# Scores of multi-head latent attention in two full passes and shared 32-row passes

## The chip, the cores and the metric

The kernel runs on one core of one Trainium2 chip. A core has TensorE (PE, the matrix unit, with a separate row PEld for loading its stationary operand), VectorE (DVE), ScalarE (ACT), GpSimd (POOL) and SyncE (SP, whose queue issues most DMAs here). The engines run side by side and wait for each other by semaphores; each works through its own instructions in order. Matmuls write to PSUM, which has eight banks of 128 partitions x 512 float32 values; everything else lies in SBUF, 128 partitions wide. The metric is the time of the whole kernel on the device in microseconds, the median of several runs.

## The reference: what is computed

Two transformer layers over 512 tokens of width 1024, each followed by a squared-ReLU MLP, and a final norm. The first layer has two attentions side by side, A (grouped-query) and B (multi-head latent). The change is in B. Its queries and keys are 96 wide: 64 without positions, and 32 with rotary positions, where the key's 32 are the same for all 8 heads.

```python
qb = (rmsnorm(cq, b_q_norm) @ b_w_uq).reshape(b, s, B_HEADS, B_NOPE + B_ROPE)      # 64 + 32
q_nope, q_rope = jnp.split(qb, (B_NOPE,), axis=-1)
q_rope = axial_rope(q_rope, row, col)
kvb = (rmsnorm(ckv, b_kv_norm) @ b_w_ukv).reshape(b, s, B_HEADS, B_NOPE + B_V)
k_nope, vb = jnp.split(kvb, (B_NOPE,), axis=-1)
k_rope = axial_rope(kr[:, :, None, :], row, col)
q_full = jnp.concatenate([q_nope, q_rope], axis=-1)
k_full = jnp.concatenate([k_nope, jnp.broadcast_to(k_rope, (b, s, B_HEADS, B_ROPE))], axis=-1)
ob = block_attention(q_full, k_full, vb, (B_NOPE + B_ROPE) ** -0.5)
```

`block_attention` is a softmax over all 512 keys. All is float32.

## The kernel before

Activations lie transposed, features on partitions and the 512 tokens along the free axis. TensorE multiplies in a rounded format, so the kernel splits each operand into a high part (rounded, by ScalarE) and a low part (the rest, by VectorE) and adds three products: high by high, high by low, low by high. `mm3` (lines 607 to 609) is these three matmuls for a projection.

PSUM is divided by tags: three banks `mm` for projections, two banks `s` for scores, two `t` for transposes, one `o` for attention outputs. A new tile of a tag takes a bank of that tag that is free.

`attend` (line 1095) goes through the heads, 8 of A and then 8 of B, with four query tiles of 128 for each. For a tile, `scores` (line 1127) multiplies queries by keys in a bank `s` (line 1131), VectorE takes the scaled row minimum and copies (line 1135), ScalarE takes the exponential (line 1137), VectorE the reciprocal of the sum (line 1138), and GpSimd scales (line 1139). Three tiles later `transpose` turns the four 128x128 blocks of the tile in a bank `t` (line 1106); ScalarE copies out the high part (line 1108) and VectorE the low part (line 1109), which empties the bank. When two tiles are turned, `values` multiplies them by the values in bank `o` (line 1119). After a head, `fold` adds the two halves of the output and splits pairs of heads.

Between tiles, `step` runs some microseconds of fill: a queue of projections, written as generators. During A it holds the rest of the input projection and then `projB(0)`, which makes q, k and v for the first four heads of B (parts `q0`, `k0`, `v0`). At tile 35 it receives the first output projection (three column blocks out of A's outputs), `projB(1)`, and the other output projections (3 and 2 column blocks). An output projection multiplies k = 0, 1 for all its columns and then k = 2, 3 column by column, and adds each column to the residual on VectorE (line 1065).

In `projB` a head pair's projection comes out with one head on partitions 0 to 63 and the other on 64 to 127. DMAs on SP's queue move them: the second head down to its own tile (lines 997 and 1019), and the rotary 32 rows below each head's 64 (lines 1000 and 1021). So a head's queries and keys take 96 partitions, high and low part side by side, and `passes` of `heads_B` (line 1184) gives the three products of 96 rows.

The order of instructions is written out by hand only in the opening and in the second layer's attention C. In `attend`, in the output projection and in the MLPs a planner orders each engine's instructions before the run: by program order as the priority, by an instruction's readiness in its own reckoning, with tiles given out as banks come free. So instructions of a later tile or of the fill may stand ahead of earlier ones. On the chip the order is fixed.

Of the kernel before, what the change touches and what calls it, by code (L numbers as in the profile page):

```python
# [35 lines left out]
def encoder_kernel(ctx: ExitStack, tc: tile.TileContext, ins, out, dbg=None):  # L36
# [36 lines left out]
        def free(self):  # L73
            give(self.i)

    def bank(tag, bufs):
        return ps.tile([P, 512], F32, tag=tag, bufs=bufs, name=nm(tag))

    def mmb():
        return bank("mm", 3)  # L80

    def sbk():
        return bank("s", 2)

    def stb():
        return bank("t", 2)

    def ob():
        return bank("o", 1)

    def scratch(dt=F32):
        return scp.tile([P, 512], dt, tag="sc", name=nm("sc"))
# [822 lines left out]
    def rotary_load():  # L915
        raw = hold["rawr"] = Slot(F32)
# [55 lines left out]
    def projB(g, last):  # L972
# [4 lines left out]

        def q_part():
            CQ = [s_.pair() for s_ in cqS]
            banks = three(3)  # L980
            for m in (2, 0, 1):
                for k in range(3):
                    hi, lo = (z[:, k % 2, m * P : (m + 1) * P] for z in weights(iq[k // 2]))
                    mm3(banks[m], hi, lo, CQ[k][:, 0, :], CQ[k][:, 1, :], k == 0, k == 2)
                    yield MM3
                if m == 2:
                    qc = scratch()
                    ACT.activation(qc, banks[2], AF.Copy)
# [12 lines left out]
            stg.free()  # L1001
            if last:
                for s_ in cqS:
                    s_.free()

        def k_part():
            CK = [s_.pair() for s_ in ckS]
            banks = three(2)
            for m in range(2):
                for k in range(2):  # L1010
                    hi, lo = (z[:, k, m * P : (m + 1) * P] for z in weights(iv))
                    mm3(banks[m], hi, lo, CK[k][:, 0, :], CK[k][:, 1, :], k == 0, k == 1)
                    yield MM3
                kn = scratch()
                DVE.tensor_tensor(kn, banks[m], hold["skvb"].t[:, 0:512], op=ALU.mult)
                K.extend(Slot() for _ in range(2))
                ka, kb = K[2 * m].pair(), K[2 * m + 1].pair()
                split(kn, ka)
                SP.dma_start(f32(kb[0:64, :, :]), f32(ka[64:128, :, :]))
                for k_ in (ka, kb):  # L1020
                    SP.dma_start(f32(k_[64:96, :, :]), f32(kst.pair()[0:32, :, :]))
            if last:
                kst.free()
                hold["skvb"].free()
                rpB.free()

# [68 lines left out]
    def attend(heads, step):  # L1095
# [29 lines left out]
                h["after"]()  # L1125

        def scores(h, i):
            s = sbk()
            pl = h["passes"](i)
            for n, (lh, rh) in enumerate(pl):  # L1130
                PE.matmul(s, lh, rh, start=n == 0, stop=n == len(pl) - 1)  # L1131
            h["done"](i)
            t = tiny(4)
            p = pp.tile([P, 512], F32, tag="p", name=nm("p"))
            DVE.tensor_tensor_reduce(p, s, zeros.to_broadcast([P, S]), op0=ALU.add, op1=ALU.min, scale=h["scale"](i),
                                     scalar=3e38, accum_out=t[:, 1:2])
            ACT.activation(p, p, AF.Exp, bias=t[:, 1:2], scale=-1.0, accum_out=t[:, 2:3])
            DVE.reciprocal(t[:, 3:4], t[:, 2:3])  # L1138
            POOL.tensor_scalar(p, p, t[:, 3:4], 1.0, op0=ALU.mult, op1=ALU.mult)  # L1139
            return p  # L1140

        for h in heads:
            for i in range(4):
                ripe = list(late_v)
                p = scores(h, i)
                if len(late_t) == 3:
                    transpose(*late_t.pop(0))
                late_t.append((h, i, p))
                if ripe:
                    values(*late_v.pop(0))  # L1150
                step(h, i)
        for x in late_t:
            transpose(*x)
            while late_v:
                values(*late_v.pop(0))
            fill.run(1.5)
# [20 lines left out]
    def heads_B(g):  # L1177
# [3 lines left out]
        for j in range(4):  # L1181
            q, k = Q[j].pair(), K[j].pair()

            def passes(i, q=q, k=k):
                ts = slice(i * P, (i + 1) * P)
                return [(q[0:96, 0, ts], k[0:96, 0, :]), (q[0:96, 1, ts], k[0:96, 0, :]),
                        (q[0:96, 0, ts], k[0:96, 1, :])]

            def done(i, j=j):
                if i == 3:  # L1190
                    Q[j].free()
                    K[j].free()
# [6 lines left out]
            yield dict(e=j % 2, done=done, after=after, scale=lambda i: hold["scB"][:, i : i + 1], passes=passes,  # L1199
                       vlhs=lambda kt, j=j: vv[kt // 2][:, kt % 2, j, :])  # L1200
# [10 lines left out]
    def step(h, i):  # L1211
# [869 lines left out]
```

## Time and profile before

| what | value |
|---|---|
| median of 3 runs | 1157.25 us (1157.03 to 1159.0) |
| the profiled execution's own time | 1158.44 us |
| its span | 1156.7 us |
| granted TensorE clock, mean | 0.998 |
| busy: PE / DVE / ACT / POOL | 1144.4 / 905.6 / 668.7 / 579.5 us |
| attention B in the span | scores from 144 to 228 us |

In the views that follow, a row of a timeline has the start, the duration, the engine, the line of the kernel, the instruction, what it writes `<-` what it reads (`s`, `t`, `o`, `mm` are PSUM tiles, `a` a slot of SBUF, `p` the softmax's tile, `whi`/`wlo` split weights), the shapes, and a count; in square brackets stands the idle time before it and what ended it. A row of groups has the count, then the busy time, the mean of one in ns, and the idle time before. `96*128 96x512` is a matmul with 96 rows of contraction and 512 columns. Matmuls overlap, so their durations are longer than their distance.

### The profile page before, as it was taken

The page shows a single profiled execution, that of the slowest core. Times are in us where ns is not written, and L with a number is a line of the kernel's source. Part 1 is how long each engine was busy: PE and PEld are TensorE (multiplying, and loading weights), DVE is VectorE, ACT ScalarE, POOL GpSimd, SP SyncE. Part 2 cuts the span into 40 slices and gives each one's busy share as a digit, 9 for nine tenths or more (in the row PEclk, how much of TensorE's full clock was granted, in tenths as well). Part 3 has the DMA queues.
Part 4 walks back from the last instruction along what each step waited for, and adds up shares of the span by engine and source line. Part 5 has one row for each costly group of instructions (what it writes and reads, how often), then busy time and mean ns, then how long its engine had stood idle before and what let it go on. Part 6 is the DMA issues. An engine that isn't in the chain of part 4 may idle for free.

```text
span 1156.7 us, 20518 instructions
## 1 busy us (share of the span) xinstructions
PE 1144.4 (99%) x7348; PEld 1022.1 (88%) x7348; DVE 905.6 (78%) x1576; ACT 668.7 (58%) x1135; POOL 579.5 (50%) x711
## 2 busy tenths in 40 slices
PE   9999999999999999999999999999999999999997
PEld 7787788888899999899988998988889999989996
DVE  6887988888877787978784666667996788698875
ACT  6677777755346668534453555555552666773445
POOL 4366252226688892378402232231388789535730
PEclk9999999999999999999999999999999999999999
DMA  7322415222523335933536574433344233372332
GB/s 234 95 79 71 106 51 142 65 64 80 169 92 96 88 99 140 270 105 101 155 92 164 143 182 127 119 108 119 101 155 128 74 90 94 74 192 70 121 121 73
DMA packets 115349, 134.36 MB, mean 116 GB/s; under 512 B 9795, under 2 KB 96752, under 8 KB 115248
## 3 DMA queue, kind: packets, MB, share of 16 engines
q1 hardware_dynamic: 110896, 120.09, 35.2%
q0 software_dynamic: 4032, 12.60, 5.4%
q8 instruction: 58, 0.95, 0.3%
q14 instruction: 43, 0.35, 0.1%
q10 hardware_dynamic: 320, 0.36, 0.1%
HBM read 110.61 MB, written 6.29 MB: 101 GB/s over the span
## 4 chain that ended last, share of the span: by engine, by line
PE 94%; DVE 2%; DMA 1%; issue 1%; ACT 1%; SPq 0%; POOL 0%; DVEq 0%; ACTq 0%; POOLq 0%
PE mm L607 8%; PE mm L608 8%; PE mm L609 8%; PE mm L451 4%; PE mm L453 4%; PE mm L452 4%; PE t L451 3%; PE t L453 3%; PE t L452 3%; PE s L1131 3%; PE o L1119 3%; PE s L451 2%; PE s L453 2%; PE s L609 2%; PE s L452 2%; PE s L607 2%
## 5 line engine op out<-in xcount | busy, mean ns | idle before, releaser
L364 DVE TENSOR_TENSOR wlo<-a,whi 128x896 fp32r<-128x896 f32 x106 | 131.9, 1248 | 56.1 <-ACT whi L363 55.5
L607 PE MATMUL mm<-a,whi 128*128 128x512 f32 x428 | 173.8, 407 | 0.2
L609 PE MATMUL mm<-a,wlo 128*128 128x512 f32 x428 | 168.9, 396 | 0.0
L608 PE MATMUL mm<-a,whi 128*128 128x512 f32 x428 | 168.9, 395 | 0.0
L363 ACT ACTIVATE whi<-a 128x896 fp32r<-128x896 f32 x106 | 100.6, 949 | 110.7 <-PE s L452 30.3
L223 DVE TENSOR_TENSOR wlo<-raw,whi 128x1024 fp32r<-128x1024 f32 (+4 forms) x97 | 111.8, 1158 | 27.6 <-ACT whi L233 27.1
L233 ACT ACTIVATE whi<-raw 128x1024 fp32r<-128x1024 f32 (+3 forms) x100 | 92.2, 924 | 69.9 <-PE s L608 24.9
L451 PE MATMUL mm<-a,whi 128*128 128x256 f32 x430 | 120.6, 280 | 0.0
L453 PE MATMUL mm<-a,wlo 128*128 128x256 f32 x430 | 120.3, 280 | 0.0
L452 PE MATMUL mm<-a,whi 128*128 128x256 f32 x430 | 120.3, 280 | 0.0
L359 POOL TENSOR_TENSOR a<-a 128x128 f32<-128x128 f32 x104 | 98.6, 948 | 8.2
L363 ACT ACTIVATE whi<-raw 128x896 fp32r<-128x896 f32 x58 | 55.1, 953 | 81.0 <-PE s L452 24.6
L358 POOL TENSOR_TENSOR a<-a 128x256 f32<-128x256 f32 x104 | 92.6, 890 | 8.2
L609 PEld LDWEIGHTS mm<-a,wlo 128*128 128x128 f32 x428 | 80.2, 188 | 18.3
L607 PEld LDWEIGHTS mm<-a,whi 128*128 128x128 f32 x428 | 80.4, 188 | 17.2 <-issue 0.9
L608 PEld LDWEIGHTS mm<-a,whi 128*128 128x128 f32 x428 | 80.7, 189 | 14.9 <-DVE a L964 0.2
L364 DVE TENSOR_TENSOR wlo<-raw,whi 128x896 fp32r<-128x896 f32 x58 | 70.8, 1230 | 26.2 <-ACT whi L363 26.1
L1139 POOL TENSOR_SCALAR p<-p,ti 128x512 f32<-128x512 f32 x64 | 45.5, 712 | 86.3 <-DVE ti L1138 62.9
L1724 POOL TENSOR_SCALAR p<-p,ti 128x256 f32<-128x256 f32 x64 | 35.5, 566 | 105.1 <-DVE ti L1723 92.1
L451 PE MATMUL t<-a,whi 128*128 128x256 f32 x312 | 87.5, 280 | 0.0
L453 PE MATMUL t<-a,wlo 128*128 128x256 f32 x312 | 87.2, 280 | 0.0
L452 PE MATMUL t<-a,whi 128*128 128x256 f32 x312 | 87.2, 280 | 0.0
(436 smaller groups left out, 3577.9 us busy)
## 6 DMA issues: line engine op xcount, KB each, us to landing
a<-in_ffn_w_up_dram SPq DMA_DIRECT2D x102, 256.0 KB, 2.8
raw<-in_ffn_w_down_dram SPq DMA_DIRECT2D x34, 512.0 KB, 4.2
raw<-in_ffn_w_down_dram SPq DMA_DIRECT2D x56, 256.0 KB, 2.7
raw<-in_od_w_qkv_dram SPq DMA_DIRECT2D x64, 128.0 KB, 2.9
raw<-in_ffn_w_up_dram SPq DMA_DIRECT2D x12, 512.0 KB, 3.9
wlo<-in_ffn_w_down_dram POOLq DMA_DIRECT2D x12, 512.0 KB, 6.3
a<-a SPq DMA_DIRECT2D x18, 256.0 KB, 3.3
bx<-a SPq DMA_DIRECT2D x32, 128.0 KB, 5.3
```

The source lines that it names most:

```text
L223: z = lambda: (eng or DVE).tensor_tensor(to, src, f32(high), op=ALU.subtract)
L233: ACT.activation(hi[:, 0:m], raw[:, 0:m], AF.Copy)
L358: held(eng.tensor_tensor(r[:, 4:6], r[:, 2:3].to_broadcast([P, 2, P]), r[:, 0:7:6], op=ALU.add))
L359: held(eng.tensor_tensor(r[:, 7], r[:, 3], r[:, 5], op=ALU.subtract))
L363: ACT.activation(hi[:, 0:896], raw[:, 128:1024], AF.Copy)
L364: DVE.tensor_tensor(lo[:, 0:896], raw[:, 128:1024], f32(hi[:, 0:896]), op=ALU.subtract)
L451: PE.matmul(o, wh, x[:, 0], start=kp == 0 and n in (0, 1, 3, 5), stop=False, skip_group_check=True)
L452: PE.matmul(o, wh, x[:, 1], start=False, stop=False, skip_group_check=True)
L453: PE.matmul(o, wl, x[:, 0], start=False, stop=kp == self.np - 1, skip_group_check=True)
L607: PE.matmul(o, wh, xh, start=first, stop=False)
L608: PE.matmul(o, wh, xl, start=False, stop=False)
L609: PE.matmul(o, wl, xh, start=False, stop=last)
```

## The change

**Scores of B.** Three products of 96 rows are 288 rows of contraction. They are packed differently: two passes of 128 rows and one of 32. The first pass has the high parts of the 64, the high part of the query's rotary 32, and its low part, against the key's high parts (the rotary high part twice). The second has the query's low 64 and high 64 against the key's high 64 and low 64. What is left is the query's rotary high part by the key's rotary low part, 32 rows. For these a tile `edge` holds, for each query tile i, the four heads' 32 rows turned by 32i partitions, so that the four tiles of one head lie in four different groups of 32 partitions; the key's rotary low part is on all four groups. At a head's first tile, four banks `s` are taken, and four 32-row matmuls, one per query tile and bank, start their sums; the two full passes of each tile are added later.

**Copies.** The operands need more moves between partitions: 7 DMAs for `edge`, 14 for the queries and 14 for the keys per group of four heads, where there were 12, and two for the rotary key. The keys' low part goes to a scratch tile first.

**Banks.** Each of the eight banks has its own tag, and each kind of tile goes round its list in turn: 3, 2, 2, 1 for `mm`, `s`, `t`, `o` as a rule, and 2, 4, 1, 1 during B. For the last three transposes of B the `t` list has a second bank, one of the four of `s`. `projB` takes its banks one at a time, and the output projections have two column blocks each, four products instead of three.

```diff
-    def bank(tag, bufs):
-        return ps.tile([P, 512], F32, tag=tag, bufs=bufs, name=nm(tag))
+    USUAL = dict(mm=[0, 1, 2], s=[3, 4], t=[5, 6], o=[7])
+    FOUR = dict(mm=[0, 1], s=[2, 3, 4, 5], t=[6], o=[7])
+    layout = [USUAL, dict(mm=0, s=0, t=0, o=0)]
+
+    def share(banks):
+        layout[:] = [banks, dict(mm=0, s=0, t=0, o=0)]
+
+    def bank(kind):
+        at = layout[0][kind]
+        n = layout[1][kind] % len(at)
+        layout[1][kind] = n + 1
+        return ps.tile([P, 512], F32, tag=f"b{at[n]}", bufs=1, name=nm(kind))
...
@@ ev_kr
         DVE.tensor_tensor(kp[0:32, 1, :], kr[0:32, :], f32(kp[0:32, 0, :]), op=ALU.subtract)
+        SP.dma_start(f32(kp[32:64, :, :]), f32(kp[0:32, :, :]))
+        SP.dma_start(f32(kp[64:128, 1, :]), f32(kp[0:64, 1, :]))
@@ projB, q_part
-            banks = three(3)
+            banks = {}
             for m in (2, 0, 1):
+                banks[m] = mmb()
...
-                    stg = Slot()
+                    stg, edge = Slot(), Slot()
+                    QKV[g]["edge"] = edge
                     split(qr, stg.pair())
+                    for i in range(4):
+                        for to, fr, m in ((32 * i, 0, 128 - 32 * i), (0, 128 - 32 * i, 32 * i)):
+                            if m:
+                                SP.dma_start(f32(edge.t[to : to + m, P * i : P * i + P]),
+                                             f32(stg.pair()[fr : fr + m, 0, P * i : P * i + P]))
...
                     split(banks[m], qa)
                     SP.dma_start(f32(qb[0:64, :, :]), f32(qa[64:128, :, :]))
+                    SP.dma_start(f32(qb[64:128, 1, :]), f32(qa[64:128, 0, :]))
+                    SP.dma_start(f32(qa[64:128, 1, :]), f32(qa[0:64, 0, :]))
                     for e, q in enumerate((qa, qb)):
                         j = 2 * m + e
-                        SP.dma_start(f32(q[64:96, :, :]), f32(stg.pair()[32 * j : 32 * j + 32, :, :]))
+                        for z in range(2):
+                            SP.dma_start(f32(q[64 + 32 * z : 96 + 32 * z, 0, :]),
+                                         f32(stg.pair()[32 * j : 32 * j + 32, z, :]))
@@ projB, k_part (its banks likewise one at a time)
-                split(kn, ka)
-                SP.dma_start(f32(kb[0:64, :, :]), f32(ka[64:128, :, :]))
-                for k_ in (ka, kb):
-                    SP.dma_start(f32(k_[64:96, :, :]), f32(kst.pair()[0:32, :, :]))
+                lo = scratch(F32R)
+                ACT.activation(ka[:, 0, :], kn, AF.Copy)
+                DVE.tensor_tensor(lo, kn, f32(ka[:, 0, :]), op=ALU.subtract)
+                for z in range(2):
+                    SP.dma_start(f32(kb[0:64, z, :]), f32(ka[64:128, 0, :]))
+                SP.dma_start(f32(ka[0:64, 1, :]), f32(ka[0:64, 0, :]))
+                for e, k_ in enumerate((ka, kb)):
+                    SP.dma_start(f32(k_[64:128, 0, :]), f32(kst.pair()[0:64, 0, :]))
+                    SP.dma_start(f32(k_[64:128, 1, :]), f32(lo[64 * e : 64 * e + 64, :]))
@@ attend
         def scores(h, i):
-            s = sbk()
+            if "edge" in h and i == 0:
+                h["s"] = [sbk() for _ in range(4)]
+                for n, (s, (lh, rh)) in enumerate(zip(h["s"], h["edge"]())):
+                    PE.matmul(s, lh, rh, start=True, stop=False)
+            s = h["s"][i] if "edge" in h else sbk()
             pl = h["passes"](i)
             for n, (lh, rh) in enumerate(pl):
-                PE.matmul(s, lh, rh, start=n == 0, stop=n == len(pl) - 1)
+                PE.matmul(s, lh, rh, start=n == 0 and "edge" not in h, stop=n == len(pl) - 1)
...
                 step(h, i)
+        share(dict(FOUR, t=[3, 6]))
         for x in late_t:
@@ heads_B
-                return [(q[0:96, 0, ts], k[0:96, 0, :]), (q[0:96, 1, ts], k[0:96, 0, :]),
-                        (q[0:96, 0, ts], k[0:96, 1, :])]
+                return [(q[:, z, ts], k[:, z, :]) for z in range(2)]
+
+            def edge(j=j):
+                e = QKV[g]["edge"].t
+                at = [32 * ((i + j) % 4) for i in range(4)]
+                return [(e[a : a + 32, P * i : P * i + P], kst.pair()[a : a + 32, 1, :]) for i, a in enumerate(at)]
...
@@ all_heads
         yield from heads_A()
+        fill.until("v0")
+        share(FOUR)
         yield from heads_B(0)
@@ step, tile 35
-            fill.add(*out_proj(w_out, 0, ok, [0, 1, 2], "out"))
+            fill.add(*out_proj(w_out, 0, ok, [0, 1], "out"))
             projB(1, True)
-            fill.add(*out_proj(w_out, 0, ok, [3, 4, 5], "out"))
-            fill.add(*out_proj(w_out, 0, ok, [6, 7], "out"))
+            for m in (2, 4, 6):
+                fill.add(*out_proj(w_out, 0, ok, [m, m + 1], "out"))
...
     fill.until("out")
+    share(USUAL)
```

More of the change, by code (lines that the diff above doesn't have):

```diff
@@ L74, in free @@
             give(self.i)
-    def bank(tag, bufs):
-        return ps.tile([P, 512], F32, tag=tag, bufs=bufs, name=nm(tag))
+    USUAL = dict(mm=[0, 1, 2], s=[3, 4], t=[5, 6], o=[7])
[8 more added lines that the diff above has]
+        return ps.tile([P, 512], F32, tag=f"b{at[n]}", bufs=1, name=nm(kind))
     def mmb():
-        return bank("mm", 3)
+        return bank("mm")
     def sbk():
-        return bank("s", 2)
+        return bank("s")
     def stb():
-        return bank("t", 2)
+        return bank("t")
     def ob():
-        return bank("o", 1)
+        return bank("o")
     def scratch(dt=F32):
@@ L1007, in k_part @@
             CK = [s_.pair() for s_ in ckS]
-            banks = three(2)
+            banks = {}
             for m in range(2):
+                banks[m] = mmb()
                 for k in range(2):
@@ L1017, in k_part @@
                 ka, kb = K[2 * m].pair(), K[2 * m + 1].pair()
-                split(kn, ka)
-                SP.dma_start(f32(kb[0:64, :, :]), f32(ka[64:128, :, :]))
-                for k_ in (ka, kb):
-                    SP.dma_start(f32(k_[64:96, :, :]), f32(kst.pair()[0:32, :, :]))
+                lo = scratch(F32R)
[7 more added lines that the diff above has]
+                    SP.dma_start(f32(k_[64:128, 1, :]), f32(lo[64 * e : 64 * e + 64, :]))
             if last:
-                kst.free()
                 hold["skvb"].free()
@@ L1197, in after @@
                         s_.free()
-            yield dict(e=j % 2, done=done, after=after, scale=lambda i: hold["scB"][:, i : i + 1], passes=passes,
+                    QKV[g]["edge"].free()
+                    if g:
+                        kst.free()
+            yield dict(e=j % 2, edge=edge, done=done, after=after, scale=lambda i: hold["scB"][:, i : i + 1], passes=passes,
                        vlhs=lambda kt, j=j: vv[kt // 2][:, kt % 2, j, :])
```

## The prediction

> **What bounds the kernel now.** I read the page first (busy shares), then the busy time by stretch around attention B, then the groups of instructions of those stretches, then the timeline, instruction by instruction. The page:
>
> ```profile
> span 1156.7 us, 20518 instructions
> PE 1144.4 (99%) x7348; PEld 1022.1 (88%) x7348; DVE 905.6 (78%) x1576; ACT 668.7 (58%) x1135; POOL 579.5 (50%) x711
> ```
>
> TensorE (PE) is never free for long, so a pass taken off it is worth its time, if nothing else sets the pace where it is taken off. The scores of attention B run from 144 to 228 us. The view by stretch, with columns as its first line says:
>
> ```profile
> core 0: us, PE busy (x) PEld busy (x) DVE busy (x) ACT busy (x) POOL busy (x), PEclk, DMA share, GB/s
> 144.00:160.00 16.00, 16.00 (x101) 13.77 (x100) 15.23 (x39) 13.26 (x31) 9.34 (x13) 1.00 0.16 54
> 160.00:190.00 30.00, 29.82 (x178) 25.64 (x177) 26.29 (x58) 21.98 (x46) 11.27 (x13) 1.00 0.43 113
> 190.00:219.00 29.00, 29.00 (x164) 24.11 (x163) 23.58 (x52) 17.86 (x38) 6.29 (x9) 1.00 0.29 87
> 219.00:229.00 10.00, 10.00 (x64) 8.17 (x63) 9.62 (x24) 7.88 (x18) 3.10 (x5) 1.00 0.23 66
> ```
>
> The granted clock is 1.00 throughout. VectorE (DVE) is busy 15.23 of 16 us (95%) at the start, 49.87 of 59 us (85%) in the middle, 9.62 of 10 us (96%) at the end. So there are two kinds of stretch: a middle in which TensorE alone is the bound, because projections fill it, and two ends with little fill, where VectorE is as full as TensorE. What the middle holds, by groups of the window 160 to 219:
>
> ```profile
> L1131 PE MATMUL s<-a,a 96*128 96x512 f32 x55 | 15.9, 398 | 0.0
> L607 PE MATMUL mm<-a,whi 128*128 128x512 f32 x36 | 15.0, 418 | 0.0
> L1106 PE MATMUL t<-cst,p 128*128 128x128 f32 x73 | 11.1, 273 | 0.0
> ```
>
> 55 score passes are recorded there (56 weight loads; one record is missing), some 18.7 of the 32 query tiles. A mean of 398 ns is the latency of one pass; what it costs in a stream is the distance of two starts. The timeline has it, and one whole step of the loop:
>
> ```profile
> 161.06 0.39 PE L608 MATMUL mm<-a,whi 128*128 128x512 f32 x1
> 161.29 0.40 PE L609 MATMUL mm<-a,wlo 128*128 128x512 f32 x1
> ...
> 162.24 0.87 PE L1131 MATMUL s<-a,a 96*128 96x512 f32 x3
> ...
> 162.94 0.60 PE L1106 MATMUL t<-cst,p 128*128 128x128 f32 x4
> ...
> 163.59 0.60 ACT L1108 ACTIVATE a<-t 128x512 fp32r<-128x512 f32 x1 [1.58 <-PE t L1106]
> ...
> 164.21 0.69 DVE L1109 TENSOR_TENSOR a<-t,a 128x512 fp32r<-128x512 f32 x1 [0.20 <-ACT a L1108]
> ```
>
> A pass of 512 columns costs 0.233 us (161.29 - 161.06), three score passes 0.70 (162.94 - 162.24). A transposed tile leaves its bank 1.96 us after its first transpose starts (164.21 + 0.69 - 162.94).
>
> **The change, part by part.**
>
> *Passes.* Per head, 12 passes over 96 rows become 8 over 128 rows and four over 32 rows in four row groups. In the middle that removes 18.7 x 0.233 = 4.4 us and adds 4.7 sets of four. No set of four row groups is in the trace. Bounds: all at once, 0.233; one after another, 4 x 0.233 = 0.93. Each needs its own weight load, and four loads with short matmuls run here:
>
> ```profile
> 166.19 0.60 PE L1106 MATMUL t<-cst,p 128*128 128x128 f32 x4
> ...
> 166.54 0.60 PE L1119 MATMUL o<-a,a 128*128 128x256 f32 x3
> ```
>
> Four transposes, each with a load of 128 columns, take 0.35 us, 0.09 each. I take a set as three such loads ahead of one pass, 3 x 0.09 + 0.233 = 0.50 us: the nearest row. 4.7 x 0.50 = 2.3, so the passes give -4.4 + 2.3 = -2.0 us (-3.3 to 0). The Trainium skill, "TensorE: Matmul & The Clock Gate", section "Measured speedup vs the span model", has four row tiles of K=32, N=512 at 3.07 times; by that a set would cost 0.93 / 3.07 = 0.30 us (an estimate) and the total below would be 0.9 us lower; no run here shows it yet.
>
> *Leaving and entering 32-row tiles.* The nearest rows are the matmuls behind four transposes of a 6-row operand:
>
> ```profile
> 59.62 0.50 PE L607 MATMUL mm<-a,whi 128*128 128x512 f32 x1
> ...
> 59.96 0.39 PE L608 MATMUL mm<-a,whi 128*128 128x512 f32 x1
> ```
>
> The first full pass takes 0.34 instead of 0.233, 0.1 more. 4.7 sets x 0.1 = +0.5 us (0 to +1).
>
> *The two ends.* The other 13 tiles lose a pass each too, but VectorE is at 95 and 96% there and loses no work (the reduction, the low part of the transposed tile, the fold all stay). I cost the gain there at nothing. The Trainium skill, "TensorEngine Tiling (Array Packing)", section "PSUM Bottleneck", states this: packing speeds up TensorE and not the emptying of PSUM, which may then be the bound. The ends agree (15.23 of 16 us of VectorE), the middle does not (49.87 of 59); if it held in the middle as well, the total below would be 2.0 us higher.
>
> *One bank for transposes instead of two.* A tile can then be transposed only when the one before has left: at best every 1.96 us. At the ends they come at:
>
> ```profile
> 145.48 0.60 PE L1106 MATMUL t<-cst,p 128*128 128x128 f32 x4
> 146.60 0.60 PE L1106 MATMUL t<-cst,p 128*128 128x128 f32 x4
> ...
> 147.69 0.59 ACT L1108 ACTIVATE a<-t 128x512 fp32r<-128x512 f32 x1
> ...
> 148.62 0.69 DVE L1109 TENSOR_TENSOR a<-t,a 128x512 fp32r<-128x512 f32 x1
> ...
> 156.90 0.60 PE L1106 MATMUL t<-cst,p 128*128 128x128 f32 x4
> ...
> 216.84 0.60 PE L1106 MATMUL t<-cst,p 128*128 128x128 f32 x4
> ...
> 230.62 0.60 PE L1106 MATMUL t<-cst,p 128*128 128x128 f32 x4
> ```
>
> From 145.48 to 156.90 there are six intervals, 1.90 us each; from 216.84 to 230.62 seven, 1.97 each. They come in pairs 1.1 us apart, which one bank forbids. Where ScalarE and VectorE have other work first, a tile stays longer: that of 146.60 leaves at 149.31, 2.71 us. Bounds for 13 intervals: 0, and 13 x (2.71 - 1.94) = +10, of which TensorE can cover some with projections pulled forward. The middle, with intervals near 3.2 us (59 / 18.3), pays nothing. I take a tenth of a microsecond per interval, nearer the lower row since VectorE's low part is early in its program: +1.5 us (0 to +6).
>
> *The projections' banks, two instead of three.* The first output projection of 3 columns becomes one of 2. Before attention A's last heads are done, it can run only its first two k:
>
> ```profile
> L607 PE MATMUL mm<-a,whi 128*128 128x512 f32 x6 | 2.6, 426 | 0.0
> L608 PE MATMUL mm<-a,whi 128*128 128x512 f32 x6 | 2.4, 397 | 0.0
> L609 PE MATMUL mm<-a,wlo 128*128 128x512 f32 x5 | 2.1, 412 | 0.0
> ```
>
> Those (window 137 to 153) are just these 3 columns x 2 k x 3 passes; they fill the poor stretch. With two columns 12 are left; the other 6 move into the TensorE-bound middle: 6 x 0.233 = +1.4 us (0 to +1.4). Four products of 2 columns instead of 3 + 3 + 2 split as many weights, so nothing else there.
>
> *Copies.* Per group of heads 12 issues on SP's queue become 35 (7 for the rotated rows, 14 for q, 14 for k), plus 2 for the rotary key: 48 more. Behind them on the same queue stand the weight loads; the first scores of the group wait for the last copies of its first keys. The last such copy of group 1, its landing time and the scores:
>
> ```profile
> 188.12 0.55 SPq L1021 DMA_DIRECT2D a<-a  x1
> ...
> 193.86 1.66 PE L1131 MATMUL s<-a,a 96*128 96x512 f32 x6
> ```
>
> ```profile
> a<-a SPq DMA_DIRECT2D x15, 128.0 KB, 2.9
> ```
>
> 188.12 + 2.9 = 191.0, 2.8 us of slack. 23 more issues at 0.5 each are 11.7 us of queue, but most go out beside the projections, from 172 us on, and the chain for the first keys stays two copies deep. I cost it at nothing, covered by that slack and by output projections; without the cover, 0.5 x 14 - 2.8 = +4 us.
>
> *Banks in fixed turn, in the whole kernel.* Until now a tile took whichever bank of its kind was free; now each kind goes round. In attention C two banks of three are taken at a time, and the turn hands out the bank that was emptied last:
>
> ```profile
> 661.44 0.40 PE L607 MATMUL mm<-a,whi 128*128 128x512 f32 x1
> 661.64 0.69 DVE L1623 TENSOR_TENSOR sc<-mm,rb 128x512 f32<-128x512 f32 x1 [0.32 <-PE mm L609]
> 662.14 0.40 PE L607 MATMUL mm<-a,whi 128*128 128x512 f32 x1
> ```
>
> The next product's second column starts at 662.14; the bank that the turn gives it is being read until 662.33. A wait of 0.2 to 0.3 us at two or three of seven products: +0.5 us (0 to +2).
>
> *Sum.* -2.0 + 0.5 + 1.5 + 1.4 + 0 + 0.5 = +1.9 us. The profiled execution took 1158.44 (span 1156.7), which gives 1160.3; it stood 1.2 over the median of the runs shown, 1157.25, so I forecast 1159.2.
>
> **Rivals.**
>
> *A, faster: the passes come off everywhere.* If the planner spreads the projections better over the ends, so that TensorE bounds all 32 tiles, 32 x 0.233 - 8 x 0.50 = 3.5 us come off, and 5.0 with sets of 0.30; the other terms fall away. For it: the 99% of TensorE, and VectorE's 74.7 of 85 us over the whole of attention B, which leave room for 5 us. Against it: the poor ends lie where no projection is ready. Time 1153.5 (1152 to 1156). It decides if transposes at the ends keep coming at under 2.0 us.
>
> *B, slower: the copies are late.* SP's queue works in order; an issue that waits for a landing (2.9 us) holds the weight loads and the next copies. From the point where the first keys of a group land more than 3 us later than now, TensorE waits at 144 us, where there is no fill. 4 us for the group 0, plus the +1.9 of the forecast without its cover: 1163 (1161 to 1166). Against it: the planner can reorder SP's issues as well.
>
> *C: the sets don't run side by side.* Either the row groups are served one after another, or the planner puts other matmuls between the four (in the poor ends it splits even a tile's three passes). Then a set costs 0.93, and the total is 4.7 x 0.43 = 2.0 us higher, 1161.2.
>
> **How the numbers follow.** The forecast has 0.45, A 0.33, B 0.14, C 0.08. A measurement tells about 0.2% (2.3 us) from no change, so "same" is 1154.9 to 1159.6. The forecast's own range is 1157 to 1162, over that border: 0.25 same, 0.20 slower. A gives 0.30 faster and 0.03 same, B and C 0.22 slower. Together 0.30, 0.28, 0.42. The range leaves out the lower part of A and the upper part of B: 1153.0 to 1164.0.
>
> **What would show it.** Groups: 64 score passes of 128 rows and 32 of 32 rows; four starts of 32-row matmuls within 0.3 us and the next full pass 0.5 us after the first. Stretch view: DVE at 95% or more at the ends still, and TensorE with idle time there for the first time; transposes never less than 1.96 us apart between 146 and 228. Waits: transposes that wait for VectorE's low part of the tile before (now L1109) appear. The sets' first full pass would start beside the last of the four if rival A's price of a set is right. The prediction is wrong if the scores of B end more than 3 us earlier (A), if the first scores of either group wait for a copy (B), or if the time moves outside of 140 to 245 us by more than 1 us, which would be the banks' fixed turn.

## The result, and the profile after

The changed kernel takes 1166.28 us (median of 4 runs, 1166.03 to 1166.67); the kernel before took 1157.26 beside it (4 runs). The ratio is 1.0075, with a 95% interval of 1.0057 to 1.0092: 9.0 us slower, outside the range of 1153.0 to 1164.0. The profiled execution took 1166.03 us, 7.6 more than the profiled one of before, which itself stood 1.2 over its median.

The page of the changed kernel, busy shares:

```profile
span 1164.3 us, 20594 instructions
PE 1147.3 (99%) x7348; PEld 1018.4 (87%) x7348; DVE 904.2 (78%) x1578; ACT 670.3 (58%) x1137; POOL 580.9 (50%) x711
```

TensorE still counts as 99% busy. A busy share doesn't tell a stream of passes from one with gaps inside; the other views must.

Where the time came up, by the starts of the same instructions in both traces:

| stretch | before | after |
|---|---|---|
| first transpose of attention A to last value product of B | 178.28 us | 184.01 us |
| from there to the first scores of attention C | 385.16 | 384.50 |
| scores of attention C | 166.13 | 168.66 |
| from there to the last product of the last MLP | 335.87 | 337.07 |

So +5.7 in attention A and B, +2.5 in attention C, which the change of scores doesn't touch, and +1.2 near the end; the rest is -1.9 in all, half of it ahead of the first transpose.

The busy time by stretch of the changed kernel, columns as in the prediction:

```profile
core 0: us, PE busy (x) PEld busy (x) DVE busy (x) ACT busy (x) POOL busy (x), PEclk, DMA share, GB/s
144.00:160.00 16.00, 15.14 (x82) 10.99 (x81) 10.80 (x29) 10.66 (x24) 6.03 (x10) 1.00 0.37 97
160.00:190.00 30.00, 29.55 (x182) 23.97 (x181) 26.50 (x61) 21.78 (x46) 10.05 (x12) 1.00 0.36 89
190.00:219.00 29.00, 28.54 (x162) 22.73 (x161) 23.34 (x50) 18.75 (x38) 6.25 (x9) 1.00 0.55 155
219.00:229.00 10.00, 9.66 (x53) 7.09 (x52) 9.12 (x23) 6.80 (x15) 3.57 (x4) 1.00 0.33 94
```

VectorE at the first end fell from 15.23 to 10.80 of 16 us: it isn't the bound there, it starves. TensorE issues 82 matmuls there instead of 101. Its groups in the window 144 to 229:

```profile
L1163 PE MATMUL s<-a,a 128*128 128x512 f32 x64 | 21.2, 415 | 0.0
L1134 PE MATMUL t<-cst,p 128*128 128x128 f32 x116 | 17.8, 274 | 0.8 <-DVE ti L1170 0.5 <-DVE a L1137 0.3
L1159 PE MATMUL s<-a,a 32*128 32x512 f32 x30 | 7.7, 493 | 0.0
```

64 full passes and 30 of the 32 small ones (two are over by 144 us): the change does what it says. How the small ones run is in the timeline, two places with the full passes around them:

```profile
162.97 0.40 PE L619 MATMUL mm<-a,wlo 128*128 128x512 f32 x1
...
163.28 0.63 PE L1134 MATMUL t<-cst,p 128*128 128x128 f32 x4
163.84 0.18 PEld L1159 LDWEIGHTS s<-a,a 32*128 32x128 f32 x1 [0.17 <-issue]
163.84 0.49 PE L1159 MATMUL s<-a,a 32*128 32x512 f32 x1
164.26 0.19 PEld L617 LDWEIGHTS mm<-a,whi 128*128 128x128 f32 x1 [0.24 <-issue]
164.26 0.50 PE L617 MATMUL mm<-a,whi 128*128 128x512 f32 x1
164.60 0.39 PE L618 MATMUL mm<-a,whi 128*128 128x512 f32 x1
...
178.56 0.39 PE L619 MATMUL mm<-a,wlo 128*128 128x512 f32 x1
178.88 0.19 PEld L1159 LDWEIGHTS s<-a,a 32*128 32x128 f32 x4 [0.36 <-issue]
178.88 0.50 PE L1159 MATMUL s<-a,a 32*128 32x512 f32 x4
179.31 0.30 PEld L1163 LDWEIGHTS s<-a,a 128*128 128x128 f32 x2 [0.24 <-issue]
179.31 0.50 PE L1163 MATMUL s<-a,a 128*128 128x512 f32 x1
...
179.65 0.39 PE L1163 MATMUL s<-a,a 128*128 128x512 f32 x1
```

At 178.88 four stand together, in one row of the view: by the trace's finer starts they are 3 ns apart. The full pass ahead of them starts at 178.56, the one behind at 179.31: 0.75 us between two full passes instead of 0.233, which is 0.52 more. The first full pass behind the set then takes 0.34 us (179.31 to 179.65) instead of 0.233, another 0.1, so the set costs 0.62 in all. The expectations below were written with 0.52, without this 0.1. At 163.84 a single one stands between a transposed tile and a projection: 0.42 us pass until the next pass, as behind the four (0.43), and that pass takes 0.34 too. The price is one of the place, not of the matmul. Its weight load is not brought forward here: it starts with its matmul after an idle 0.17 or 0.36, and the first full load behind it after 0.24, while the load of a full pass behind a full pass runs beside it. In the order of TensorE's instructions the 32 small matmuls stand in 17 places, ten of them single, not in eight.

The Trainium skill, "TensorEngine Tiling (Array Packing)", section "Key Properties", says that a change of the tiling mode, unlike a change of the tile, drains TensorE. The idle ahead of both loads is what that looks like here; that section gives no price.

The waits of TensorE in attention C, window 600 to 800, of the changed kernel:

```profile
PE mm L617 <- DVE ti L1766: 0.9, 1, 0.9
PE mm L1723 <- DVE sc L1682: 0.9, 2, 0.7
PE mm L617 <- DVE sc L1682: 0.7, 1, 0.7
```

Before, TensorE had only these there:

```profile
PE s L1720 <- DMA a<-sc: 0.4, 1, 0.4
PE t L636 <- DVE r L1607: 0.2, 1, 0.2
```

The first three are 2.5 us in which projections wait for VectorE. Line 1682 reads a projection's bank (`sc` from `mm`). The runs turn and turn_only below show that it is the bank they wait for.

### The profile page after: what moved, and what is told of

Its sections match the earlier page's. It is cut to its first block, busy times and chain, and to the rows that moved or that the text cites. A ratio compares the mean times of both kernels' runs of the same rounds, so it can differ in the third digit from the quotient of the medians.

```text
span 1164.3 us, 20594 instructions
## 1 busy us (share of the span) xinstructions
PE 1147.3 (99%) x7348; PEld 1018.4 (87%) x7348; DVE 904.2 (78%) x1578; ACT 670.3 (58%) x1137; POOL 580.9 (50%) x711
## 4 chain that ended last, share of the span: by engine, by line
PE 91%; DVE 5%; DMA 2%; issue 1%; ACT 1%; SPq 0%; DVEq 0%; POOL 0%; ACTq 0%; POOLq 0%
PE mm L617 8%; PE mm L618 8%; PE mm L619 8%; PE mm L461 4%; PE mm L462 4%; PE mm L463 4%; PE t L461 3%; PE t L462 3%; PE t L463 3%; PE s L461 2%; PE s L462 2%; PE s L463 2%; PE s L617 2%; PE s L619 2%; PE s L618 2%; PE o L1147 2%
## 5 line engine op out<-in xcount | busy, mean ns | idle before, releaser
L368 POOL TENSOR_TENSOR a<-a 128x256 f32<-128x256 f32 x104 | 97.9, 942 | 8.2
```

Of the source, the lines that this page charges most:

```text
L368: held(eng.tensor_tensor(r[:, 4:6], r[:, 2:3].to_broadcast([P, 2, P]), r[:, 0:7:6], op=ALU.add))
```

## Experiments

Fourteen kernels, each timed against the kernel before on the same chip (1157.3 to 1157.6 us there).

### The turn of the banks, and the places of the sets

**turn**: the changed kernel, where outside attention B every tile gets the bank that it had before, out of a list by kind (`GIVEN`).

```
+    GIVEN = dict(
...
+        b = GIVEN[kind][i] if layout[0] is USUAL else at[n]
+        return ps.tile([P, 512], F32, tag=f"b{b}", bufs=1, name=nm(kind))
```

> The changed kernel, but outside attention B each PSUM tile gets the very bank that it had in the kernel before. Theory (the fixed turn costs 2.5 us in attention C and 1.2 us in the last MLP): 3.7 us less than the changed kernel, about 1162.5 us, with the 1.1, 0.8, 0.4 and 0.8 us waits of attention C and the 1.4 us wait of the last MLP gone. Rival (these waits come from the planner's other order, or everything is lost inside attention B): within 1 us of 1166.3.

Measured 1161.78 us, ratio 1.0039 (1.0024 to 1.0054): 4.5 less than the changed kernel. The three waits in attention C are gone, and its scores take 165.72 us: 2.9 of the 4.5 lie there. A and B take 0.2 us less; where the rest lies the trace doesn't show, for the profiled execution took 1163.24, 1.5 over the median.

**whole**: the changed kernel, where the four small matmuls begin with the bank that comes free last and are kept in the order of the program.

```
-                for n, (s, (lh, rh)) in enumerate(zip(h["s"], h["edge"]())):
-                    PE.matmul(s, lh, rh, start=True, stop=False)
+                four = list(zip(h["s"], h["edge"]()))
+                for n, (s, (lh, rh)) in enumerate(four[3:] + four[:3]):
+                    m = PE.matmul(s, lh, rh, start=True, stop=False)
+                    if n:
+                        tc.keep_in_program_order(m)
```

> The changed kernel, but the four 32-row matmuls of a head are emitted with the bank that comes free last first, and each of the others is pinned behind the one before. They then stand in 11 places instead of 17. Theory (a place costs 0.52 us, whether one matmul stands there or four): 6 x 0.52 = 3.1 us less, 1163.2 us. Rival 1 (a 32-row matmul costs a pass of its own wherever it stands): no change, 1166.3. Rival 2 (waiting for the last bank costs more than the places saved): 1167 to 1169.

Measured 1163.32, ratio 1.0049 (1.0034 to 1.0064): -3.0 for 11 places instead of 17, 0.5 us each, a little under the 0.62 of the trace.

**both**: the two edits together.

> Both edits together. Theory (two separate causes, which add): 1166.3 - 3.7 - 3.1 = 1159.5 us. If they are one cause, no better than the better of the two.

Measured 1159.81, ratio 1.002 (1.0011 to 1.0029). The two add up nearly: -4.5 and -3.0 alone, -6.5 together. From turn to both the same six places are worth 2.0, 0.33 each. That a place costs less in the runs than by its starts may come from places at the ends, where TensorE waits for other engines anyway; no run shows it.

**turn_only**: the kernel before, with the turn and nothing else.

```
+    USUAL = dict(mm=[0, 1, 2], s=[3, 4], t=[5, 6], o=[7])
...
+        at = layout[0][kind]
+        n = layout[1][kind] % len(at)
```

> The kernel before with one thing changed: every kind of tile takes its banks in fixed turn, three, two, two and one as before. Scores, copies and projections are those of before. Theory (the turn alone makes attention C's projections wait for a bank that is still being read, as the waits there show in the changed kernel): +2.5 to +4.5 us, 1160 to 1162, with waits at 620 to 780 us and attention C 2 to 3 us longer. Rival (the turn costs something only together with the other order that attention B leaves behind): 1157.3, within 1 us.

Measured 1161.72, ratio 1.0037 (1.0024 to 1.005): +4.4 from the other end. Attention C takes 169.06 us (+2.9), A and B 179.53 (+1.3). Its waits in the window 600 to 800 are those of the changed kernel:

```profile
PE mm L617 <- DVE ti L1733: 0.9, 1, 0.9
PE mm L1690 <- DVE sc L1649: 0.9, 2, 0.6
PE mm L617 <- DVE sc L1649: 0.6, 1, 0.6
```

The 1.3 us of A and B are there when the scores of B begin (1.3 at the 29th of 64 transposed tiles, 1.2 at the last), so the turn costs nothing inside B. So half of the nine microseconds have nothing to do with the scores of B.

### What the passes are worth, and the copies

**copies**: the kernel before with the copies and operands of the change, and still three passes per tile: two full ones and one over 96 rows, whose product is that of other heads' leftover rows, so that the scores are not the reference's. Banks are those of before.

```
+                return [(q[:, 0, ts], k[:, 0, :]), (q[:, 1, ts], k[:, 1, :]), (e[0:96, ts], kst.pair()[0:96, 1, :])]
```

> The kernel before with its banks, but with the changed kernel's 35 copies per group and operands; per tile the two full passes and, as a third, one of 96 rows that adds products of other heads, so the scores are not those of the reference; the passes are as many and as long as before. Theory (the copies hide): 1157.6 to 1158.6 us. Rival (copies late at the heads of B): 1161 or more, with a wait of TensorE for a copy.

Measured 1158.82, ratio 1.0011 (1.0001 to 1.0021). A and B take 178.36 us, as before (178.28): the copies are hidden where they are made. The +1.5 lies elsewhere. Its profiled execution has +2.8 between the last value product of B and attention C, and there this wait, which neither the kernel before nor two_usual (next) has:

```profile
PE mm L453 <- DVE wlo L364: 1.7, 1, 1.7
```

It is a product of the MLP that waits for VectorE to split weights, far from the copies. The profiled execution took 1160.66, 1.8 over the median, so whether the other executions have this wait isn't shown.

**two_usual**: the same with the third pass left out, which leaves the query's rotary high part by the key's rotary low part out of the scores.

```
-                return [(q[:, 0, ts], k[:, 0, :]), (q[:, 1, ts], k[:, 1, :]), (e[0:96, ts], kst.pair()[0:96, 1, :])]
+                return [(q[:, z, ts], k[:, z, :]) for z in range(2)]
```

> As 'copies', but the third pass is left out, so the 32 remaining rows are not added at all: 32 passes less, no bank split, no 32-row matmul. If TensorE bounds all of B: 32 x 0.233 = 7.5 us under 'copies', about 1150. By the prediction's two ends (no gain where VectorE is at 95%): 18.7 x 0.233 = 4.4 us under it, about 1153.5.

Measured 1152.45, ratio 0.9955 (0.9939 to 0.997): 4.9 under the kernel before and 6.4 under copies, whose +1.5 isn't placed. Inside A and B the traces of copies and two_usual differ by 4.7 us (178.36 and 173.66). I take 4.9 for 32 passes, 0.15 of their 0.233 us each; 6.4 would be 0.20. TensorE is busy in nearly all of attention B, the ends too:

```profile
144.00:160.00 16.00, 15.56 (x99) 12.71 (x98) 14.44 (x37) 12.45 (x29) 8.20 (x12) 1.00 0.36 104
160.00:190.00 30.00, 30.00 (x186) 25.86 (x185) 27.71 (x62) 22.58 (x48) 11.31 (x13) 1.00 0.40 97
190.00:219.00 29.00, 28.44 (x162) 23.32 (x161) 24.82 (x61) 21.08 (x44) 7.95 (x12) 1.00 0.52 155
219.00:229.00 10.00, 10.00 (x67) 8.61 (x65) 9.28 (x20) 7.23 (x16) 3.42 (x5) 1.00 0.14 38
```

TensorE issues 99 matmuls at the first end, with a third of the score passes gone (101 before): other work moved in. Where the gain arises can be read from the transposed tiles, which go in the same order in both traces. At the 29th of 64, where B begins, two_usual is not ahead of copies (-0.1 us); at the 38th, behind the first end, it is ahead by about 1 us, at the 56th, behind the middle, by 4.8, at the last by 4.7. So the first end gains a little, and the last end gains no time, though seven other matmuls more are done by then.

### The banks of attention B

**banks**: scores, passes and copies of before; the bank split of the change in B (2, 4, 1, 1), with its two-column output projections; the banks of before elsewhere.

```
+        fill.until("v0")
+        share(FOUR)
...
-            fill.add(*out_proj(w_out, 0, ok, [0, 1, 2], "out"))
+            fill.add(*out_proj(w_out, 0, ok, [0, 1], "out"))
```

> The kernel before, with its three passes of 96 rows and its 12 copies per group, but with the changed kernel's banks in attention B (two for projections, four for scores, one for transposes) and its output projections of two columns; outside B each tile has the bank it had before. Theory (what is left in 'both', 1159.8 us against 1157.6 although 11 places at 0.52 us cost less than the 32 passes saved, is the price of these banks): 4 to 5 us over before, about 1162. Rival (the copies cost it): 1157.6, within 1 us.

Measured 1161.34, ratio 1.0033 (1.0021 to 1.0045): +4.0. Its two parts alone:

**one_t**: one transpose bank, three projection banks, three-column output projections.

```
+    FOUR = dict(mm=[0, 1, 2], s=[3, 4, 5], t=[6], o=[7])
```

> The kernel before (three score passes per tile, its copies, three-column output projections, its banks outside attention B) with one bank for transposes in attention B instead of two; the bank goes to the scores. Of the +4.0 us that both bank changes gave together: theory (a tile can be transposed only when the one before has left, and the ends have no other work) +2.5 to +3, 1160; rival (the transposes find their bank free, the cost is the projections') +0.5 or less, 1157.8.

Measured 1162.08, ratio 1.004 (1.0025 to 1.0055): +4.7.

**two_mm**: two projection banks, two transpose banks, two-column output projections.

```
+    FOUR = dict(mm=[0, 1], s=[2, 3, 4], t=[5, 6], o=[7])
```

> The kernel before (three score passes per tile, its copies, its banks outside attention B) with two banks for projections in attention B instead of three, and output projections of two columns each; transposes keep two banks, the scores have three. Theory (six passes move from the poor stretch into the full one): +1 to +1.4, 1158.5. Rival (two banks make each projection wait for the emptying of the one before): +3 to +4, 1161.

Measured 1157.92, ratio 1.0004 (0.9994 to 1.0013): +0.6, not to be told from nothing.

So the price is that of the single transpose bank. The timeline of one_t at the first end shows the cycle that it forces, transposes, ScalarE's copy and VectorE's low part:

```profile
147.70 0.63 PE L1128 MATMUL t<-cst,p 128*128 128x128 f32 x4
148.37 0.60 ACT L1130 ACTIVATE a<-t 128x512 fp32r<-128x512 f32 x1 [0.27 <-PE t L1128]
149.00 0.69 DVE L1131 TENSOR_TENSOR a<-t,a 128x512 fp32r<-128x512 f32 x1
...
149.93 0.60 PE L1128 MATMUL t<-cst,p 128*128 128x128 f32 x4
150.57 0.60 ACT L1130 ACTIVATE a<-t 128x512 fp32r<-128x512 f32 x1 [0.91 <-PE t L1128]
151.20 0.69 DVE L1131 TENSOR_TENSOR a<-t,a 128x512 fp32r<-128x512 f32 x1
...
162.06 0.63 PE L1128 MATMUL t<-cst,p 128*128 128x128 f32 x4
```

The tile of 147.70 leaves at 149.69 and the next one starts at 149.93, one at a time. From 147.70 to 162.06 there are six intervals of 2.39 us; between the same tiles they were 1.90 before, so this end takes 2.9 us more. At the other end the seven intervals from 219.79 to 235.28 take 15.49 us, where they took 13.78 before (216.84 to 230.62 in the prediction's rows), 1.7 more. Together that is 4.6 us, about what was measured, 0.36 for each of 13 intervals.

### The price of a 32-row place

**full**: the changed kernel, where the small matmuls run over all 128 rows (the sums then hold other heads' leftover rows): no change of form.

```
-                return [(e[a : a + 32, P * i : P * i + P], kst.pair()[a : a + 32, 1, :]) for i, a in enumerate(at)]
+                return [(e[:, P * i : P * i + P], kst.pair()[:, 1, :]) for i, a in enumerate(at)]
```

> The changed kernel, with the four 32-row matmuls of each head replaced by matmuls over 128 rows of the same tiles, so the scores of attention B are not those of the reference. TensorE then never leaves the 128-row form in B. Theory (17 places at 0.52 us are 9.0 us with the recorded gaps; 32 full passes at 0.233 are 7.5): about 1.5 us less, 1164.8 us. Rival (the 32-row matmuls are as cheap as one pass of 0.233 a place, 4 us in all): 3.5 us more, 1169.8 us.

Measured 1163.15, ratio 1.0049 (1.0033 to 1.0066): -3.1, twice what was expected. With the 0.62 us of a place instead of 0.52, the same sum gives it: 17 x 0.62 - 32 x 0.233 = 3.1. 32 full passes one after another are cheaper than 32 small ones in 17 places.

**two_split**: both without the small matmuls (what two_usual leaves out of the scores is left out here), with the bank split kept.

> As 'both', but the four 32-row matmuls are left out and the first full pass opens the sum, so the 32 remaining rows are not added: the bank split and the copies stay. Theory (each of the 11 places costs 0.52 us and nothing covers it): 5.7 us under 'both', 1154.1. If the bank split sets the pace of B and not TensorE's work: less than 2 us under 'both', 1158 or more.

Measured 1154.48, ratio 0.9977 (0.9967 to 0.9986): 5.3 under both, 0.48 for each of 11 places; and 2.0 over two_usual, so with two passes the bank split costs half of what it does with three. (Its ten executions lie between 1153.8 and 1156.7; the two slowest have mean clocks of 0.997 and 0.996; see eight.)

**eight**: both, with the second to fourth small matmul at high priority, so that eight whole sets are left.

```
+                four = four[3:] + four[:3]
+                PE.matmul(four[0][0], *four[0][1], start=True, stop=False)
+                with tc.high_priority():
+                    for s, (lh, rh) in four[1:]:
+                        tc.keep_in_program_order(PE.matmul(s, lh, rh, start=True, stop=False))
```

> The kernel with the usual banks outside attention B and the sets' matmuls pinned behind each other, with the second to fourth matmul of a set now at high priority, so that all eight sets stand whole: 8 places of 32-row matmuls instead of 11. Theory (a place costs 0.5 us, however many matmuls stand in it): three places fewer, -1.5 us, 1158.3. Rival (what costs time at the sets is waiting until four score banks are free at once, and a whole set waits for the last of them): no gain or a loss, 1159.8 or more.

Measured 1162.26, ratio 1.0042 (1.0027 to 1.0057): 2.4 slower than both. The rival's sign was right; I had not expected what the stretch view shows:

```profile
154.00:156.00 2.00, 1.64 (x12) 1.28 (x11) 1.24 (x5) 1.13 (x4) 0.69 (x1) 1.00 0.00 0
156.00:158.00 2.00, 0.63 (x4) 0.42 (x4) 1.24 (x3) 1.87 (x4) 0.69 (x1) 1.00 0.00 0
158.00:160.00 2.00, 0.66 (x4) 0.52 (x5) 1.94 (x6) 1.34 (x3) 0.21 (x1) 1.00 0.00 0
160.00:161.00 1.00, 1.00 (x10) 1.00 (x9) 0.74 (x2) 0.60 (x1) 0.78 (x1) 0.89 0.00 0
161.00:163.00 2.00, 2.00 (x7) 1.50 (x7) 1.16 (x4) 0.82 (x2) 0.00 (x0) 0.50 0.00 0
163.00:164.00 1.00, 1.00 (x6) 1.00 (x5) 0.44 (x2) 0.04 (x1) 0.40 (x1) 0.50 0.00 0
164.00:165.00 1.00, 1.00 (x5) 0.76 (x5) 0.39 (x1) 1.00 (x3) 0.30 (x1) 0.91 0.00 0
```

The longest wait in it is a value product's, for ScalarE's exponential:

```profile
PE o L1158 <- ACT p L1184: 1.8, 1, 1.8
```

TensorE is busy for 1.29 of the 4 us from 156 to 160, and then its granted clock is 0.50: 0.2 us of the stretch to 161, all of the next three, 0.2 of the last, 3.4 us at half speed, 1.7 lost. All four executions of eight have a mean clock of 0.996 or 0.997, most of both 0.998 or 0.999. With 1.7 taken off, eight is still 0.7 us over both: three places fewer gained nothing that is left at the end. The Trainium skill, "TensorE: Matmul & The Clock Gate", section "What's actually happening", has a gate that halves the clock after an idle window of some 3.4 us and opens it after a busy one; length and ratio agree here, though TensorE was not idle throughout. The profiled execution of two_split has the same 3.4 us from 158.3 on; those of both, of turn and of the changed kernel have a clock of 1.00 throughout these stretches.

**eight_tiny** and **both_tiny**: eight and both, with each small matmul replaced by a full 128-row one of 64 columns, whose result is written over, so that the sets and their banks stay and the form goes; the leftover rows are out of the scores.

```
+                four = [(s, (lh, rh[:, 0:64])) for s, (lh, rh) in zip(h["s"], (h["passes"](n)[0] for n in range(4)))]
...
-                PE.matmul(four[0][0], *four[0][1], start=True, stop=False)
+                PE.matmul(four[0][0][:, 0:64], *four[0][1], start=True, stop=True)
```

> The kernel with eight whole sets, with each 32-row matmul replaced by a full 128-row one of 64 columns, whose result the first full pass overwrites: the sets still stand together and wait for four score banks, and no other tile form is entered. It leaves the 32 rows out of the scores. Four such matmuls should take 4 x 0.09 = 0.35 us, as four transposes do, 2.8 us for eight sets; without any set the time was 1154.5. Theory (a whole set is dear because it waits until four banks are free at once): 1160 to 1161, most of the 1162.3 stays. Rival (what is dear is the 32-row form itself): 1154.5 + 2.8 = 1157.3 or less.

> The kernel with the usual banks outside attention B and the sets' matmuls pinned behind each other (11 places, 1159.8 us), with the same replacement: full 128-row matmuls of 64 columns in place of the 32-row ones, which leaves the 32 rows out of the scores. If only the 32-row form costs (0.52 us a place), 5.3 us go and 32 x 0.09 = 2.8 us come: 1157.3. If the waiting for banks costs at these 11 places as well, 1158.5 to 1159.5.

Measured 1156.21, ratio 0.9984 (0.9975 to 0.9994), and 1155.77, ratio 0.9983 (0.9973 to 0.9993). In both kernels the four stand together, in eight places. A set of these isn't free, here in eight_tiny from 163.31 to 163.67:

```profile
163.08 0.39 PE L630 MATMUL mm<-a,wlo 128*128 128x512 f32 x1
163.31 0.19 PE L1171 MATMUL s<-a,a 128*128 128x64 f32 x1
163.34 0.50 PE L1174 MATMUL s<-a,a 128*128 128x64 f32 x3
163.67 0.71 PE L1178 MATMUL s<-a,a 128*128 128x512 f32 x2
```

0.36 us a set, and the first full pass behind it takes 0.32 (163.67 to 163.99) instead of 0.233: 0.44 in all, 3.6 for eight by the starts. In the runs they cost 1.7 and 1.3 over two_split. So waiting for four banks is cheap, and the theory of eight_tiny's expectation falls: dear are the 32-row matmuls, with what the planner makes of them. With them instead of the 64-column ones the time is 4.0 us longer in both (11 places) and 6.1 in eight, 1.7 of which is the clock. By the starts alone it should be 11 x 0.62 - 3.6 = 3.2 in both; in eight 8 x 0.62 - 3.6 = 1.4 and the 1.7 of the clock. That leaves 0.8 us in both and 3.0 in eight. The traces show where they lie: from 156 to 160 us TensorE is idle for 1.2 us in both and 0.5 in both_tiny, for 2.7 in eight and 0.4 in eight_tiny. The planner's orders differ there; why they do, no run shows.

## Why the prediction was wrong

The runs, put in a row, lead from one kernel to the other: 1157.3, -4.9 with the copies and 32 passes less (two_usual), +2.0 with the bank split (two_split), +5.3 with small matmuls in 11 places (both), +2.0 with 17 places (turn), +4.5 with the turn of the banks: 1166.2. Each step is a difference of two medians, so the row adds up by itself; what it shows is the size of each step. I forecast +1.9 and measured +9.0. Two terms of my sum failed: the sets of 32-row matmuls, 2.8 in the sum and 7.3 in the runs, and the banks' turn, 0.5 in the sum and 4.5 in the runs.

- **Banks in fixed turn**, +0.5 (0 to +2): measured +3.5 to +4.5. The mechanism was right and in the place that I named: a projection of attention C waits for the bank emptied last. The term was mis-sized: I took 0.2 to 0.3 us from one pair of rows, in which the reading was nearly over; the waits in the trace are up to 0.9, at four places, 2.5 together, and in turn_only another 1.3 us come up in attention A and B, where I looked for none.
- **A set's price**, 0.50 and 0.1 for leaving: measured 0.62 for a whole set with entering and leaving. The size was right; its unit was not. It falls due per place, and I counted 4.7 sets where the order has 17 places. I had the planner's splitting as rival C, but gave it a set that is served one after another (0.93), 4.4 us in all; in the trace the row groups do run side by side, and the splitting costs more than that. 32-row matmuls cost 5.3 + 2.0 = 7.3 us here, and the passes that they replace gave 4.9: in the sum, the -2.0 + 0.5 is +2.4.
- **The two ends gain nothing**: nearly right. Two_usual gains 4.9 of 7.5, where I counted 4.4 (6.4 if the unplaced +1.5 of copies belonged to it). By the transposed tiles the middle gains 3.8, the first end about 1 and the last end nothing. So VectorE's 95% was no limit at the first end. In the changed kernel VectorE fell to 10.80 of 16 us there, so my sign of 95% did not come.
- **One transpose bank**, +1.5 (0 to +6): +4.7 alone (one_t). The mechanism held: between 146 and 228 us of the changed kernel no two tiles' transposes start closer than 2.1 us. By itself the term was mis-sized, since I added 0.1 per interval and in one_t it is 0.36. With two passes the whole bank split costs 2.0 (two_split against two_usual), less than my 1.5 + 1.4 for its two parts; this sum came near although its parts did not, which is luck.
- **Two projection banks**, +1.4: +0.6 in two_mm, which the noise covers.
- **Copies**, nothing: right in attention B (178.36 against 178.28), and rival B falls; no wait of TensorE for a DMA stands in the window 100 to 245 of the changed kernel. The +1.5 of the whole run stays open, with a wait of 1.7 us in the MLP as a part of it in the profiled execution.
- **Rival A** was right that the planner moves other work to where the passes came off, and had no place for the three costs above. Its mark, transposes under 2.0 us apart at the ends, didn't come.
- My sign for the fixed turn, more than 1 us outside of 140 to 245 us, came: +2.5 in attention C. The +1.2 in the last MLP is not explained: a wait of 1.2 us for VectorE at 1100 us, 1.1 in turn and none before, stays when the turn is undone. It is smaller in other orders of the same work (0.5 in both, 0.4 in eight).

None of the kernels that compute the reference's scores is faster than the one before. With the turn undone, the passes would have to pay for the transpose bank and for eight to eleven places of the other form, and they don't (1159.8).

## What to carry to other kernels

Count the places where small-row matmuls stand between full ones in the order as it is written out, not the sets: here each costs some 0.6 us by its starts and 0.3 to 0.5 in the runs, whether one or four run in it, and by the starts a lone one costs more than two full passes. Give out banks as they come free unless every user of the turn has been looked at; a helper shared by the whole kernel moves time far from the edit. And a second buffer that looks idle on average can be what lets a tile start before the last one has left: read it from the intervals of starts, not from the mean load.

## What the runs showed of the hardware

- Four 32-row matmuls on four row groups start 3 ns apart and end together (0.49 to 0.50 us each). Four full passes take 0.93 us and a set with its entry and exit 0.62, so the set is 1.5 times as fast. The Trainium skill, "TensorE: Matmul & The Clock Gate", section "Measured speedup vs the span model", has about 4 ns per tile and 3.07 times; the spacing agrees, and the factor is not reached here between full passes.
- At the changes of form shown above, the weight load did not run beside the matmul ahead: it stood idle for 0.17 and 0.36 us ahead of a first small one and for 0.24 ahead of a first full one, and the first full pass took 0.34 us instead of 0.233.
- TensorE, busy for 1.29 of 4 us in eight, was then given half its clock for 3.4 us; in two_split it had been busy for 2.0 of the last 3.4 us, and in both a stretch of 3.4 us with 2.1 us of work brought no such cut. No single wait in eight's stretch was longer than 1.8 us.
